# Three handovers in another order: one output-projection pass for two, a weight sum made one product earlier, and the retention's last two sweeps inside the norm's plan

## The chip, the cores and the metric

The kernel runs on one core of a Trainium2 chip. The metric is the device time of one execution in microseconds; the kernel before took 2762.98 us (median of three runs, 2762.88 to 2763.43).

## What is computed

A two-layer decoder trunk over 1024 positions of width 1024, in float32. Cut to what matters here:

```python
# layer 0: dilated attention beside a gated short convolution
x = x + concat([attention, conv_mixer], -1) @ even_w_out
x = x + ffn(rms_norm(x, ffn_norm[0]), 0)
# layer 1: retention with an output gate
x = x + (silu(xn @ wg) * group_norm(retention(q, k, v))) @ ret_wo
x = x + ffn(rms_norm(x, ffn_norm[1]), 1)

def ffn(xn, l):                       # D_FF = 2816
    u = causal_dwconv(xn @ w_up[l], conv_w[l])      # width 3
    g, val = split(u, 2, axis=-1)
    return (silu(g) * val) @ w_down[l]
```

So the products that the change touches are the output projection of layer 0, FFN 0's and 1's first block and down product, and the retention's output projection.

## The kernel before

**Numbers.** Every matmul operand is two float32r parts, high and low. `split` (L107) makes them: ScalarE (ACT) casts the high part (L109), and GpSimd (POOL) or VectorE (DVE) subtracts it for the low part (L110). `hilo` puts both parts in a buffer "hl" (7 of them) or in one that is passed in. `PASSES` (L47) lists the three matmuls that one product of parts takes. The residual x stays in SBUF as `xb`, eight row tiles of 128 positions.

**The output projections.** `sweep` (L296) goes over row tiles and the two halves of 512 columns: per pair of parts of the contraction three matmuls (L303) into one of four PSUM banks "o", then one addition of the bank to `xb` on DVE (L308). It yields after every row tile, so two additions. `project` (L568) is a sweep over the mixer's parts `mix[j]`; parts (1,3) and (5,7) ran earlier, beside the attention. `wo_sweep` (L1082) is one for a head of the retention; g is the half of the head's value dimension.

**The norms.** `Norming.play` walks a plan, a string of steps. "q2" makes the sums of squares of row-tile pair 2 (ACT L163, then the reciprocal root on POOL, L152 and L153); "r2" makes its normed rows in tiles "u" (DVE L172, two pieces of 512 per row tile, four per pair); "t2" turns them with PE (L179, sixteen transposes into four banks "b"); "c2" combines them into seven operand tiles `xc` (`combine`, L184: one ACT copy, L196 to L201 and three L110 on DVE, four L110 on POOL). "a", "A" and "b", "B" are the halves of a "q" and an "r". "s", "d" and "h" advance something else: "s" a sweep by two row tiles, "d" a sweep or the down product by so many steps, "h" the first FFN block by so many of its products. `PLAN` stands in front of FFN 0, `PLAN_DOWN` at the end of FFN 0's down product, `PLAN_LATE` in front of FFN 1.

**The FFN.** A block is `strassen` (L206): seven products (L220) over seven `xc` operands instead of eight; the first block runs in two halves of 256 columns so that it can start while later pairs are still being normed. The convolution (L892) of the first block follows it. The down product is `down_steps` (L719): five groups of 11 steps (products 1 and 2, 5 and 6, 3 and 7, 4, and the second half of 4), each step loading weight rows into "raw" buffers (5), making sums on DVE (L758), splitting, and multiplying (L826); a group ends with additions to `xb` (L834). The loop loads 4 steps ahead and makes operands 2 ahead.

**What sets the order.** The Python order of these calls gives each instruction its place, and a list scheduler puts the instructions on each engine's queue, which runs in that order. Buffers of one tag are reused when free, and a later user waits. DMA loads go out on SyncE (SP), stores on ACT's queue.

**The retention.** `last_block` (L1098) is the last projection block, with the first unit's loads, rotations (L979) and transposes between its products. Scores are L1012, masked with the tile "tri" on DVE (L1017). `gated` (L1068) turns a unit's output, multiplies it by the gate and splits it for `wo_sweep`.

## Time and profile before

| | us |
|---|---|
| profiled execution, device time | 2762.86 |
| its span, first to last instruction | 2761.1 |
| PE busy | 2675.4 |
| DVE busy | 1953.2 |
| ACT busy | 1191.6 |
| POOL busy | 754.2 |
| mean granted TensorE clock | 0.988 |

Between the profiled execution's time and its span lie 1.8 us. How to read what follows: a row of the timeline gives the start and length in us of a run of instructions of one kind, the engine, the source line, the operation, output and inputs by tile name, how many, and in brackets how long the engine had idled before it and what ended that idle time. A row of the windows gives, for a stretch of the span, the busy time of each engine with its number of instructions, the clock that TensorE was granted (1.00 is full), and the DMA engines' busy share. PE stands for TensorE's matmuls and PEld for its weight loads.

### The profile page before, as it was taken

To read this page: it belongs to the slowest core of one execution; us is meant where nothing else is said; L and a number is where in the kernel's file an instruction comes from. 1 tells how busy PE (TensorE), PEld (TensorE's weight loads), DVE (VectorE), ACT (ScalarE), POOL (GpSimd) and SP (SyncE) were. 2 spreads that over 40 slices of the span, in tenths; PEclk is the share of its full clock that TensorE was granted. 3 is DMA by queue.
4 is the path that set the end of the run, shared out by engine and by line. 5 is a ranking of instruction groups with operands and counts; after the bars stand their busy time and mean duration, and the time that the engine had idled before them with its cause. 6 is when DMAs were issued, how large, how long until landed. Compare 5 with 4: busy or idle time off the path is not lost.

```text
span 2761.1 us, 33920 instructions
## 1 busy us (share of the span) xinstructions
PE 2675.4 (97%) x12249; PEld 2151.1 (78%) x12249; DVE 1953.2 (71%) x2930; ACT 1191.6 (43%) x2030; POOL 754.2 (27%) x619
## 2 busy tenths in 40 slices
PE   8999999889999999989999999999998999999999
PEld 6877777678888877867888887788877888887887
DVE  4247676788787888785444435888778878787886
ACT  4344453355454444363333333333325545444444
POOL 6721113342222200033212122555555222221000
PEclk9999999999999999999999999999999999999999
DMA  5310002022222264433333335544321222224636
GB/s 170 102 47 28 24 31 80 27 78 76 86 75 87 74 244 160 138 118 117 103 111 103 111 104 175 167 158 137 100 77 50 78 86 75 87 74 168 210 122 212
DMA packets 250268, 294.73 MB, mean 107 GB/s; under 512 B 14288, under 2 KB 169076, under 8 KB 250100
## 3 DMA queue, kind: packets, MB, share of 16 engines
q1 hardware_dynamic: 233676, 238.55, 27.5%
q10 hardware_dynamic: 16424, 54.01, 5.1%
q8 instruction: 96, 1.57, 0.2%
q14 instruction: 72, 0.59, 0.1%
HBM read 234.31 MB, written 58.20 MB: 106 GB/s over the span
## 4 chain that ended last, share of the span: by engine, by line
PE 75%; DVE 12%; POOL 5%; issue 3%; DMA 3%; ACT 2%; SPq 0%; DVEq 0%; POOLq 0%; ACTq 0%
PE o L220 23%; PE b L220 22%; PE o L826 7%; PE b L826 6%; PE u L433 4%; PE n L382 2%; PE u L382 2%; PE o L303 2%; POOL hl L110 2%; DVE xb L308 2%; PE pv L503 1%; PE u L303 1%; PE s L472 1%; PE pt L515 1%; DVE u L172 1%
## 5 line engine op out<-in xcount | busy, mean ns | idle before, releaser
L110 POOL TENSOR_TENSOR hl<-raw,hl 128x512 fp32r<-128x512 f32 x347 | 499.3, 1448 | 1316.7 <-ACT hl L109 1293.4
L220 PE MATMUL b<-xc,hl 128*128 128x512 f32 (+1 forms) x2988 | 684.1, 388 | 1.4 <-POOL xc L110 0.9
L220 PE MATMUL o<-xc,hl 128*128 128x512 f32 (+1 forms) x2904 | 672.8, 391 | 10.3 <-ACT u L275 3.0
L220 PEld LDWEIGHTS b<-xc,hl 128*128 128x128 f32 x2988 | 548.5, 188 | 130.2 <-POOL xc L110 1.2
L220 PEld LDWEIGHTS o<-xc,hl 128*128 128x128 f32 x2904 | 537.9, 191 | 136.9 <-ACT u L275 3.6
L110 DVE TENSOR_TENSOR hl<-s,hl 128x512 fp32r<-128x512 f32 x325 | 225.1, 696 | 359.1 <-ACT hl L109 359.1
L109 ACT CAST hl<-raw 128x512 fp32r<-128x512 f32 (+1 forms) x424 | 257.9, 612 | 428.7 <-PE o L303 79.5
L892 DVE SCALAR_TENSOR_TENSOR u<-u,cc,u 128x1022 f32<-128x1022 f32 (+1 forms) x176 | 303.2, 1744 | 1.1
L109 ACT CAST hl<-s 128x512 fp32r<-128x512 f32 x325 | 199.7, 619 | 154.4 <-PE b L220 42.5
L433 PE MATMUL u<-xT,hl 128*128 128x512 f32 x576 | 172.8, 416 | 0.0
L308 DVE TENSOR_TENSOR xb<-xb,o 128x512 f32<-128x512 f32 x176 | 114.9, 678 | 21.9 <-PE o L303 21.6
L433 PEld LDWEIGHTS u<-xT,hl 128*128 128x128 f32 x576 | 99.4, 192 | 23.8 <-issue 9.5
L890 ACT ACTIVATE u<-u,cc 128x1024 f32<-128x1024 f32 x88 | 101.1, 1151 | 38.5 <-DVE u L287 30.2
L826 PE MATMUL o<-hl,hl 128*128 128x512 f32 x444 | 110.7, 393 | 2.4 <-DVE hl L110 1.6
L303 PE MATMUL o<-hl,ya 128*128 128x512 f32 x384 | 97.8, 406 | 5.1 <-DVE xb L308 5.1
L826 PEld LDWEIGHTS o<-hl,hl 128*128 128x128 f32 x444 | 83.0, 188 | 23.0 <-DVE hl L110 3.4
L893 ACT ACTIVATE u<-u 128x1024 f32<-128x1024 f32 x44 | 46.7, 1062 | 110.3 <-DVE u L892 110.2
L303 PEld LDWEIGHTS o<-hl,ya 128*128 128x128 f32 x384 | 73.4, 194 | 22.2 <-DVE xb L308 5.4
L152 POOL TENSOR_SCALAR rr<-ss 128x1 f32<-128x1 f32 (+1 forms) x48 | 13.4, 279 | 269.5 <-ACT s L163 250.5
L303 PE MATMUL o<-hl,yb 128*128 128x512 f32 x336 | 81.2, 397 | 0.0
L826 PE MATMUL b<-hl,hl 128*128 128x512 f32 x312 | 76.5, 392 | 1.1 <-DVE xb L834 1.0
L110 POOL TENSOR_TENSOR xc<-u,xc 128x512 fp32r<-128x512 f32 x48 | 66.4, 1411 | 35.7 <-DVE u L199 19.8
(207 smaller groups left out, 4011.8 us busy)
## 6 DMA issues: line engine op xcount, KB each, us to landing
raw<-in_ffn_w_up SPq DMA_DIRECT2D x176, 256.0 KB, 3.1
raw<-in_ffn_w_down SPq DMA_DIRECT2D x176, 256.0 KB, 3.1
scr<-u ACTq DMA_DIRECT2D x48, 512.0 KB, 2.8
hs<-u ACTq DMA_DIRECT2D x44, 512.0 KB, 2.7
h<-hs SPq DMA_DIRECT2D x44, 512.0 KB, 5.9
raw<-in_even_w_in SPq DMA_DIRECT2D x73, 256.0 KB, 2.9
raw<-in_ret_wo SPq DMA_DIRECT2D x64, 256.0 KB, 3.0
xb<-in_x SPq DMA_DIRECT2D x16, 512.0 KB, 3.2
```

What stands on the lines that cost most here:

```text
L109: act.copy(hi, src)
L110: (eng or pool).tensor_tensor(lo, src, f(hi), ALU.subtract)
L172: dve.scalar_tensor_tensor(xn[:, cs], xt[:, cs], r, g[i], ALU.mult, ALU.mult)
L220: pe.matmul(u, hl[:, ws, k * P : (k + 1) * P], xc[b][:, xs, k, cols_], start=(first and k == 0 and i == 0), stop=(k == 3 and i == 2), skip ...
L303: pe.matmul(o, lhs[j](ls, t), ws[j][hf][:, w, :], start=(j == 0 and i == 0), stop=(j == n - 1 and i == 2),)
L308: dve.tensor_tensor(xs, xs, o, ALU.add)
L382: pe.matmul(banks[t], xT[:, xs, k, t0 : t0 + P], hl[:, ws, :], start=(k == 0 and i == 0), stop=(k == KT - 1 and i == 2),)
L433: pe.matmul(u, hl(ws, k), xT[:, xs, k, hf * 512 : (hf + 1) * 512], start=(k == 0 and i == 0), stop=(k == KT - 1 and i == 2),)
L826: pe.matmul(o, l[:, ls, c * P : (c + 1) * P], r[:, ws, :], start=(start and i == 0), stop=(stop and i == 2), skip_group_check=True,)
L890: act.mul(c, u, wcol(2, jj))
L892: dve.scalar_tensor_tensor(c[:, d:], u[:, :-d], wcol(2 - d, jj), c[:, d:], ALU.mult, ALU.add)
L893: act.activation(cs[0], cs[0], AF.Silu)
```

## The change

It has five parts.

1. The plan strings are written in another order.
2. Layer 0's output projection runs passes (0,2), then (4,6) inside `PLAN`; before, (0,2) and (4,) ran by themselves and (6,) inside `PLAN`. The part `mix[4]` now lives in two "u" tiles, and "u" has five buffers instead of four.
3. In the down product the sum t4 = b21 − t4, its weight load and its store move from the group of product 4 into that of products 3 and 7. Two steps of product 4 share one "hl" buffer for their quarter-width operands, their t4 splits use "hl" buffers only, and from the third group's end on operands are made three steps ahead.
4. The last unit's gated output goes into an "h" tile and two "u" tiles, and both of its sweeps run inside `PLAN_LATE`, advanced by "d"; before, the first of them ran ahead of the plan.
5. The tile "tri" comes from the norm's "g" buffers, which are free earlier than its old place.

```diff
...
-PLAN = "s0 q0 s1 q1 r0 t0 s2 q2 c0 r1 t1 s3 q3 c1 r2 t2 c2 r3 h4 t3 c3 h4"
-PLAN_LATE = "t0 c0 s2 q2 t1 s3 q3 c1 r2 t2 c2 r3 t3 h4 c3 h4"
+PLAN = "s0 q0 s1 q1 r0 t0 s2 q2 c0 r1 s3 q3 t1 c1 h1 r2 t2 h1 c2 r3 h1 t3 h1 c3 h4"
+PLAN_LATE = "d1 t0 d1 c0 r1 d1 t1 d1 c1 d2 q2 h1 r2 d1 t2 d1 q3 h1 c2 r3 h1 t3 h1 c3 h4"
...
-    for js in ((0, 2), (4,)):
-        run(project(js, ORDER, o_bank))
+    run(project((0, 2), ORDER, o_bank))
...
-    nrm.play(PLAN, xc, project((6,), ORDER, o_bank), head[0])
+    nrm.play(PLAN, xc, project((4, 6), ORDER, o_bank), head[0])
...
-            return rhs(1, 1, k), rhs(0, 1, k)
...
+            return rhs(1, 1, k), rhs(0, 1, k), rhs(1, 0, k)
...
+            p7 = both(s3), both(t3)
             t4 = left[k][:, :HALF]
             add(t4, b21, t4, ALU.subtract)
-            p4 = quarter(right[k][:, HALF : HALF + 256]), both(t4)
             act.dma_start(out=ts[k], in_=t4)
-            return [p4]
+            return [p3, p7]
...
+            if k % 2 == 0:
+                pair.append(wp.tile([P, 2, 512], "hl", HL, F32R))
+            hl = pair[-1][:, :, k % 2 * 256 : k % 2 * 256 + 256]
...
+            while made_to[0] < min(n + AHEAD + (n >= 3 * KH), len(steps) - 1):
...
+        if last:
+            t = h_tile()
+            yT = [t[:, :, i * HALF : (i + 1) * HALF] for i in range(2)]
+            yT += [u_tile().bitcast(F32R).rearrange("p (s t) -> p s t", s=2) for _ in range(2)]
...
-        unit0["tri"] = rt[0].tile([P, HALF], "tri")
+        unit0["tri"] = wk.tile([P, HALF], "g", 2)
...
-            nrm.play("q0 r0 q1 r1")
+            nrm.play("q0 r0 q1")
...
-    run(wo_sweep(half, h, yT, 0, ORDER[4:]))
...
-    nrm.play(PLAN_LATE, xc, wo_sweep(half, h, yT, 1, ORDER[4:]), head[0])
+    nrm.play(PLAN_LATE, xc, chain(*[wo_sweep(half, h, yT, g, ORDER[4:]) for g in range(2)]), head[0])
```

What this does to the queues shows at three places. The first is DVE's queue in front of FFN 0 in the kernel before, from the seventh addition of pass (6,): `o` are banks of the projection, `u` normed rows, `rr` reciprocal roots, `b` banks of transposes.

```order
684 L308 TENSOR_TENSOR xb_71<-xb_71,o_4975 128x512
685 L308 TENSOR_TENSOR xb_71<-xb_71,o_4980 128x512
686 L172 SCALAR_TENSOR_TENSOR u_4997<-xb_71,rr_4956,g_4919 128x512
687 L172 SCALAR_TENSOR_TENSOR u_4997<-xb_71,rr_4956,g_4920 128x512
688 L172 SCALAR_TENSOR_TENSOR u_5000<-xb_71,rr_4962,g_4919 128x512
689 L172 SCALAR_TENSOR_TENSOR u_5000<-xb_71,rr_4962,g_4920 128x512
690 L308 TENSOR_TENSOR xb_71<-xb_71,o_5023 128x512
691 L308 TENSOR_TENSOR xb_71<-xb_71,o_5028 128x512
692 L308 TENSOR_TENSOR xb_71<-xb_71,o_5033 128x512
693 L308 TENSOR_TENSOR xb_71<-xb_71,o_5038 128x512
694 L196 TENSOR_TENSOR u_5055<-u_5056,b_5003 128x512
695 L198 TENSOR_TENSOR u_5056<-b_5018,u_5056 128x512
```

In the changed kernel the same queue at the same point of the norm, with the banks of pass (4,6):

```order
665 L308 TENSOR_TENSOR xb_71<-xb_71,o_4870 128x512
666 L172 SCALAR_TENSOR_TENSOR u_4942<-xb_71,rr_4889,g_4830 128x512
667 L308 TENSOR_TENSOR xb_71<-xb_71,o_4878 128x512
668 L172 SCALAR_TENSOR_TENSOR u_4942<-xb_71,rr_4889,g_4831 128x512
669 L308 TENSOR_TENSOR xb_71<-xb_71,o_4898 128x512
670 L172 SCALAR_TENSOR_TENSOR u_4945<-xb_71,rr_4895,g_4830 128x512
671 L308 TENSOR_TENSOR xb_71<-xb_71,o_4906 128x512
672 L172 SCALAR_TENSOR_TENSOR u_4945<-xb_71,rr_4895,g_4831 128x512
673 L308 TENSOR_TENSOR xb_71<-xb_71,o_4914 128x512
674 L308 TENSOR_TENSOR xb_71<-xb_71,o_4922 128x512
675 L196 TENSOR_TENSOR u_5012<-u_5013,b_4948 128x512
676 L198 TENSOR_TENSOR u_5013<-b_4963,u_5013 128x512
```

The normed rows of pair 0 stood together between additions of pass (6,); now they alternate with the additions of the merged pass, and combining tile 0 (L196 is its first step on DVE) comes after eight additions of the last pass instead of twelve.

The second place is PE's queue near the end of FFN 0's down product, before: the second tile's transposes among the steps of product 4 (the bank `o` and the operand buffers name the step).

```order
1715 L826 MATMUL o_8521<-hl_10421,hl_10418 128x512 x3
1716 L826 MATMUL o_8522<-hl_10421,hl_10418 128x512 x3
1717 L826 MATMUL o_8521<-u_10437,u_10434 128x512 x3
1718 L826 MATMUL o_8522<-u_10437,u_10434 128x512 x3
1719 L826 MATMUL o_8521<-hl_10494,hl_10491 128x512
1720 L826 MATMUL o_8522<-hl_10494,hl_10491 128x512
1721 L826 MATMUL o_8521<-hl_10494,hl_10491 128x512 x2
1722 L826 MATMUL o_8522<-hl_10494,hl_10491 128x512 x2
1723 L179 MATMUL b_10535<-ident_67,u_10349 128x128 x4
1724 L179 MATMUL b_10540<-ident_67,u_10367 128x128 x4
1725 L179 MATMUL b_10545<-ident_67,u_10349 128x128 x4
1726 L179 MATMUL b_10550<-ident_67,u_10367 128x128 x4
```

And in the changed kernel:

```order
1723 L833 MATMUL o_8490<-hl_10409,hl_10406 128x512 x3
1724 L833 MATMUL o_8491<-hl_10409,hl_10406 128x512 x3
1725 L833 MATMUL o_8490<-hl_10445,hl_10406 128x512
1726 L833 MATMUL o_8491<-hl_10445,hl_10406 128x512
1727 L179 MATMUL b_10501<-ident_67,u_10333 128x128 x4
1728 L179 MATMUL b_10506<-ident_67,u_10336 128x128 x4
1729 L179 MATMUL b_10511<-ident_67,u_10333 128x128 x4
1730 L179 MATMUL b_10516<-ident_67,u_10336 128x128 x4
1731 L833 MATMUL o_8490<-hl_10445,hl_10406 128x512 x2
1732 L833 MATMUL o_8491<-hl_10445,hl_10406 128x512 x2
```

The operands now come from "hl" buffers alone, one of them (`hl_10406`) serving two steps. Behind these transposes 34 matmuls of the down product remain, where 30 remained before.

The third place is DVE's queue in front of FFN 1, before: the eight pieces of normed rows of pairs 0 and 1 between the additions of two sweeps.

```order
2192 L308 TENSOR_TENSOR xb_71<-xb_71,o_17313 128x512
2193 L172 SCALAR_TENSOR_TENSOR u_17340<-xb_71,rr_17334,g_17321 128x512
2194 L172 SCALAR_TENSOR_TENSOR u_17340<-xb_71,rr_17334,g_17322 128x512
2195 L172 SCALAR_TENSOR_TENSOR u_17355<-xb_71,rr_17346,g_17321 128x512
2196 L172 SCALAR_TENSOR_TENSOR u_17355<-xb_71,rr_17346,g_17322 128x512
2197 L172 SCALAR_TENSOR_TENSOR u_17358<-xb_71,rr_17352,g_17321 128x512
2198 L172 SCALAR_TENSOR_TENSOR u_17358<-xb_71,rr_17352,g_17322 128x512
2199 L308 TENSOR_TENSOR xb_71<-xb_71,o_17381 128x512
2200 L308 TENSOR_TENSOR xb_71<-xb_71,o_17389 128x512
```

And in the changed kernel:

```order
2175 L308 TENSOR_TENSOR xb_71<-xb_71,o_17273 128x512
2176 L172 SCALAR_TENSOR_TENSOR u_17297<-xb_71,rr_17288,g_17282 128x512
2177 L172 SCALAR_TENSOR_TENSOR u_17300<-xb_71,rr_17294,g_17281 128x512
2178 L172 SCALAR_TENSOR_TENSOR u_17300<-xb_71,rr_17294,g_17282 128x512
2179 L308 TENSOR_TENSOR xb_71<-xb_71,o_17388 128x512
2180 L308 TENSOR_TENSOR xb_71<-xb_71,o_17396 128x512
2181 L196 TENSOR_TENSOR u_17440<-u_17441,b_17404 128x512
2182 L198 TENSOR_TENSOR u_17441<-b_17419,u_17441 128x512
2183 L199 TENSOR_TENSOR u_17440<-b_17419,u_17440 128x512
```

Four pieces instead of eight stand ahead of the first additions of the last unit's sweeps (`o_17388` is the first of them, as `o_17381` was), and combining tile 0 begins behind two of their additions instead of eight.

More of the change, by code (lines that the diff above doesn't have):

```diff
@@ L561, in gather @@
         for j in js:
-            hl = into.tile([P, 2, T], "h" if j == 6 else f"ab{j}", dt=F32R)
-            split(hl[:, 0, :], hl[:, 1, :], xb[:, j, :] if src is None else src, dve if j in (1, 5, 0, 6) else None)
+            if j == 4:
+                hl = [mix["mp"].tile([P, T], "u", 5, F32R) for _ in range(2)]
+            else:
+                t = into.tile([P, 2, T], "h" if j == 6 else f"ab{j}", dt=F32R)
+                hl = [t[:, s, :] for s in range(2)]
+            split(*hl, xb[:, j, :] if src is None else src, dve if j in (1, 5, 0, 6) else None)
             mix[j] = hl
@@ L569, in project @@
         return sweep(
-            [lambda s, t, h=mix[j]: h[:, s, t * P : (t + 1) * P] for j in js],
+            [lambda s, t, h=mix[j]: h[s][:, t * P : (t + 1) * P] for j in js],
             [w_rows(w_out, (j // 2) + (4 if j % 2 else 0)) for j in js], tiles, bank, after,
@@ L657, in u_tile @@
     def u_tile():
-        return mp.tile([P, T], "u", 4)
+        return mp.tile([P, T], "u", 5)
     def h_tile():
@@ L706, in tile @@
         def tile(shape, tag, bufs):
-            return (mp if tag == "u" else wk).tile(shape, tag, bufs)
+            return u_tile() if tag == "u" else wk.tile(shape, tag, bufs)
     xc = xc_tiles()
@@ L748, in hl_tile @@
                 return wp.tile([P, 2, 512], "hl", HL, F32R)
-            return mp.tile([P, 2, 512], "u", 4, F32R)
+            return mp.tile([P, 2, 512], "u", 5, F32R)
         def both(src, eng=dve):
@@ L793, in make_37, with quarter, make_4 @@
             t3 = add(s_tile(), b22, b12, ALU.subtract)
-            return [p3, (both(s3), both(t3))]
-        def quarter(src):
-            hl = hl_tile()
-            split(hl[:, 0, :256], hl[:, 1, :256], src, dve)
+            p7 = both(s3), both(t3)
+            t4 = left[k][:, :HALF]
+            add(t4, b21, t4, ALU.subtract)
+            act.dma_start(out=ts[k], in_=t4)
+            return [p3, p7]
+        pair = []
+        def quarter(src, k):
+            if k % 2 == 0:
+                pair.append(wp.tile([P, 2, 512], "hl", HL, F32R))
+            hl = pair[-1][:, :, k % 2 * 256 : k % 2 * 256 + 256]
+            split(hl[:, 0, :], hl[:, 1, :], src, dve)
             return hl
         def load_4(k):
-            return (rhs(1, 0, k),)
-        def make_4(k, b21):
-            t4 = left[k][:, :HALF]
-            add(t4, b21, t4, ALU.subtract)
-            p4 = quarter(right[k][:, HALF : HALF + 256]), both(t4)
-            act.dma_start(out=ts[k], in_=t4)
-            return [p4]
+            return ()
+        def make_4(k):
+            return [(quarter(right[k][:, HALF : HALF + 256], k), hilo(left[k][:, :HALF], None, dve))]
         def load_4b(k):
@@ L818, in make_4b @@
         def make_4b(k, t4, a22):
-            return [(quarter(a22[:, :256]), both(t4))]
+            return [(quarter(a22[:, :256], k), hilo(t4, None, dve))]
         x, y = [o_bank() for _ in range(4)], [b_bank() for _ in range(4)]
@@ L1068, in gated @@
     def gated(h, y, gt, last):
-        yT = [yp.tile([P, 2, 2, HALF], "ya", dt=F32R)]
-        yT.append(
-            h_tile().rearrange("p s (c t) -> p s c t", c=2) if last else yp.tile([P, 2, 2, HALF], "yb", dt=F32R)
-        )
+        if last:
+            t = h_tile()
+            yT = [t[:, :, i * HALF : (i + 1) * HALF] for i in range(2)]
+            yT += [u_tile().bitcast(F32R).rearrange("p (s t) -> p s t", s=2) for _ in range(2)]
+        else:
+            t = [yp.tile([P, 2, 2, HALF], f"y{i}", dt=F32R) for i in range(2)]
+            yT = [t[c // 2][:, :, c % 2] for c in range(4)]
         for c in range(4):
@@ L1083, in lhs @@
         def lhs(j):
-            return lambda s, t: yT[g][:, s, j, (t - 4 * half) * P : (t - 4 * half + 1) * P]
+            return lambda s, t: yT[2 * g + j][:, s, (t - 4 * half) * P : (t - 4 * half + 1) * P]
         return sweep(
```

15 lines of the change are left out of this document (7 added, 8 removed).

## The prediction

> **What bounds the kernel now.** I read the page first, then busy time by window, the waits of TensorE (PE), and the timelines of PE and VectorE (DVE) in the stages that wait.
>
> ```profile
> span 2761.1 us, 33920 instructions
> ...
> PE 2675.4 (97%) x12249; PEld 2151.1 (78%) x12249; DVE 1953.2 (71%) x2930; ACT 1191.6 (43%) x2030; POOL 754.2 (27%) x619
> ...
> L308 DVE TENSOR_TENSOR xb<-xb,o 128x512 f32<-128x512 f32 x176 | 114.9, 678 | 21.9 <-PE o L303 21.6
> ```
>
> PE is busy for 2675.4 of 2761.1 us. The change keeps all of its matmuls, so nothing can be won where PE never pauses. The rows below give, for each stretch: PE, PE load, DVE, ACT and POOL busy time, then the granted TensorE clock, the DMA share and GB/s.
>
> ```profile
> 510.00:590.00 80.00, 62.80 (x347) 54.76 (x346) 75.87 (x108) 37.20 (x70) 35.09 (x36) 0.85 0.15 44
> 540.00:560.00 20.00, 13.50 (x64) 12.04 (x64) 17.80 (x24) 8.58 (x17) 9.12 (x10) 0.58 0.05 14
> 640.00:680.00 40.00, 40.00 (x172) 32.18 (x171) 32.13 (x35) 19.08 (x28) 9.71 (x6) 1.00 0.26 83
> 1080.00:1120.00 40.00, 40.00 (x176) 32.63 (x175) 37.58 (x63) 17.57 (x30) 0.00 (x0) 1.00 0.46 147
> 1120.00:1160.00 40.00, 40.00 (x175) 32.65 (x174) 28.32 (x46) 16.38 (x29) 0.00 (x0) 1.00 0.30 99
> 1196.00:1269.00 73.00, 58.35 (x330) 47.46 (x329) 64.15 (x96) 41.37 (x84) 33.27 (x27) 0.93 0.33 98
> 1220.00:1240.00 20.00, 16.56 (x76) 12.55 (x77) 19.18 (x29) 12.18 (x25) 8.48 (x6) 0.85 0.48 142
> 1700.00:1760.00 60.00, 52.20 (x248) 41.83 (x247) 47.86 (x69) 26.86 (x43) 31.30 (x26) 0.94 0.64 224
> 2055.00:2128.00 73.00, 59.84 (x343) 52.55 (x343) 64.72 (x93) 37.68 (x72) 40.05 (x38) 0.88 0.17 48
> ```
>
> The steady FFN stretch (640 to 680) is plain PE work: 172 matmuls in 40.00 us, 0.2325 us each. Four stretches are not: the norm in front of FFN0 (510 to 590, PE idle 17.2 us), the handover from FFN0's down product to the retention projections (1196 to 1269, 14.7 us), the entry to the retention (1700 to 1760, 7.8 us) and the norm in front of FFN1 (2055 to 2128, 13.2 us). Together they hold 52.8 of PE's 85.7 idle us. In the first, DVE is busy for 75.87 of 80 us: DVE's list sets that stage's length.
>
> **The change, part by part.** *Norm in front of FFN0.* Passes (4,) and (6,) of the output projection become one pass (4,6). Each pass adds 16 tiles into xb on DVE (L308); 48 additions become 32, and the matmuls stay. These are DVE's and PE's rows there:
>
> ```profile
> 511.72 16.42 DVE L308 TENSOR_TENSOR xb<-xb,o 128x512 f32<-128x512 f32 x25
> 528.05 2.73 DVE L172 SCALAR_TENSOR_TENSOR u<-xb,rr,g 128x512 f32<-128x512 f32 x4
> 530.70 2.47 DVE L308 TENSOR_TENSOR xb<-xb,o 128x512 f32<-128x512 f32 x4
> 533.09 0.68 DVE L196 TENSOR_TENSOR u<-u,b 128x512 f32<-128x512 f32 x1
> ...
> 536.75 1.80 DVE L172 SCALAR_TENSOR_TENSOR u<-xb,rr,g 128x512 f32<-128x512 f32 x1
> ...
> 544.88 0.68 DVE L196 TENSOR_TENSOR u<-u,b 128x512 f32<-128x512 f32 x1
> ...
> 557.69 0.69 DVE L196 TENSOR_TENSOR u<-u,b 128x512 f32<-128x512 f32 x1 [2.20 <-ACT u L195]
> ...
> 569.60 0.68 DVE L196 TENSOR_TENSOR u<-u,b 128x512 f32<-128x512 f32 x1
> ...
> 590.20 2.48 DVE L892 SCALAR_TENSOR_TENSOR u<-u,cc,u 128x1023 f32<-128x1023 f32 x2
> ```
>
> ```profile
> 521.66 7.60 PE L303 MATMUL o<-hl,h 128*128 128x512 f32 x32
> ...
> 530.47 1.47 PE L179 MATMUL b<-ident,u 128*128 128x128 f32 x12
> ...
> 538.70 0.63 PE L179 MATMUL b<-ident,u 128*128 128x128 f32 x4 [3.95 <-DVE u L172]
> 541.96 2.82 PE L179 MATMUL b<-ident,u 128*128 128x128 f32 x12 [2.63 <-DVE u L172]
> 546.66 0.58 PE L220 MATMUL o<-xc,hl 128*128 128x256 f32 x1 [1.88 <-ACT xc L109]
> ```
>
> Four additions from 530.70 end where L196 starts at 533.09: 2.39 us, 0.60 each when DVE is not held. The 25 at 511.72 begin with the last addition of pass (0,2), which both orders have, so this is a common anchor. Combining tile 1 starts at 544.88, 33.16 us behind it, with 33 additions, 8 pieces of normed rows and 7 pieces of combining tile 0 between. In the changed order the same span holds 17 additions, the same 15 other pieces and two more pieces of weight work: 16 × 0.60 less, 2 × 0.60 more, so −8.4 us. Two things must not hold DVE back. PE: pass (6,) starts at 521.66 and pass (4,) is 48 matmuls, so pass (0,2) ended near 521.66 − 48 × 0.2325 = 510.5; 96 matmuls from there end at 532.8, before the 536.5 that DVE's sum gives. And the pieces that stand behind one another: with six matmuls per addition (1.40 us against 0.60) DVE has 0.8 us free per tile beside the pass, into which the rows and the first combine fall. Further on, the 2.20 us in which DVE waited for ACT ahead of combining tile 2 should be filled, since rows, sums and splits of FFN weights have moved ahead: −2.2. Sum −10.6. Nothing gained (0 of the 2.2, a further 2 us held by the split that gives back the u buffers) is −6; all 4.1 us of DVE's idle gone and the additions at 0.68 (16 × 0.68 + 4.1) is −15. The fifth u buffer is there because mix[4] occupies two of them to the end of the pass; if r1's second row must wait for the POOL split of tile 0, that is inside the −6.
>
> *FFN0's down product.* The sum t4 = b21 − t4 moves from the fourth product to the third, with its load on SP and its store on ACT. DVE then does seven pieces per step there instead of six, at about 0.6 us in a step of 24 × 0.2325 = 5.58 us. The window at 1080 has three loads per step and DVE at 37.58 of 40 us with PE at 40.00; the one at 1120 has two and 28.32. So room exists: cost 0, up to +2. In the fourth product one DVE piece per step goes, but two steps share a buffer.
>
> The handover after it has a shorter way to tile 0 (transposes one step earlier) and rows spread between down steps:
>
> ```profile
> 1215.35 0.66 PE L179 MATMUL b<-ident,u 128*128 128x128 f32 x4 [1.19 <-DVE xc L110]
> 1216.95 0.63 PE L179 MATMUL b<-ident,u 128*128 128x128 f32 x4 [0.94 <-DVE xc L110]
> 1218.60 0.76 PE L179 MATMUL b<-ident,u 128*128 128x128 f32 x4 [1.03 <-DVE xc L110]
> ...
> 1228.01 1.19 PE L826 MATMUL o<-hl,hl 128*128 128x512 f32 x4 [1.55 <-DVE hl L110]
> ...
> 1252.23 1.98 PE L179 MATMUL b<-ident,u 128*128 128x128 f32 x12 [2.28 <-DVE u L172]
> ```
>
> DVE's list is nearly the same length; it is idle for 73 − 64.15 = 8.9 us of this stretch. The three waits of tile 1 come to 3.2 us; the new order puts less between tile 0's rows and its combine, but more after. I take −2, with −5 (all 3.2 and most of the 2.28) and +2 (shared buffers hold a split) as ends.
>
> *Entry to the retention.* The triangle's load comes earlier, and three score matmuls now stand among the last projection block's matmuls.
>
> ```profile
> 1720.50 2.32 DVE L110 TENSOR_TENSOR qk<-kf,qk 128x1024 fp32r<-128x1024 f32 x1
> ...
> 1725.63 3.92 PE L1012 MATMUL b<-qk,qk 128*128 128x512 f32 x24
> ```
>
> They need what DVE finishes at 1722.8; with 24 matmuls (5.6 us) behind them they would be reached near 1720, so PE may stop for 2.8 us, or win it back as the scores end sooner. I take 0, ends −2 and +3.
>
> *Norm in front of FFN1.* One of the last two passes of the retention's output projection ran before the norm, with eight pieces of normed rows ahead of its additions on DVE. Both passes now run inside the plan.
>
> ```profile
> 2060.25 1.41 DVE L172 SCALAR_TENSOR_TENSOR u<-xb,rr,g 128x512 f32<-128x512 f32 x2 [0.44 <-POOL rr L153]
> 2062.11 3.41 DVE L172 SCALAR_TENSOR_TENSOR u<-xb,rr,g 128x512 f32<-128x512 f32 x2 [0.44 <-POOL rr L153]
> 2065.44 2.47 DVE L308 TENSOR_TENSOR xb<-xb,o 128x512 f32<-128x512 f32 x4
> ```
>
> ```profile
> 2066.17 8.66 PE L303 MATMUL o<-hl,ya 128*128 128x512 f32 x24 [5.13 <-DVE xb L308]
> ...
> 2076.11 5.83 PE L303 MATMUL o<-hl,h 128*128 128x512 f32 x24
> ...
> 2101.18 1.09 PE L179 MATMUL b<-ident,u 128*128 128x128 f32 x4 [4.16 <-DVE u L172]
> 2104.44 2.82 PE L179 MATMUL b<-ident,u 128*128 128x128 f32 x12 [2.17 <-DVE u L172]
> ```
>
> PE stopped for 5.13 us because no bank was free, and the 24 matmuls behind it took 8.66 instead of 5.83 us: 8.0 us. Here no DVE work goes; DVE's idle time, 73 − 64.72 = 8.3 us, is all that can be won without shortening its list. I take −7, ends −4 (the later sum of squares of pair 3 leaves a wait near tile 3) and −11 (the halved clock behind 4.16 goes too).
>
> Other edits (POOL's orders, the tag names, the earlier buffers) lie beside PE at 40.00 in its windows: 0. Sum: −10.6 − 2 + 0 − 7 ± 0 = −19.6, about −20 us. The profiled run took 2762.86 us, 0.12 under the median of 2762.98; the forecast is 2743. The best ends give −15 − 5 − 2 − 11 = −33, the worst −6 + 2 + 2 + 3 − 4 = −3.
>
> The clock deserves a look: 540 to 560 ran at 0.58, behind stalls of 3.95 and 2.63 us. The Trainium skill, TensorE: Matmul & The Clock Gate, section "What's actually happening", says that PE's clock halves after about 3.4 us of idleness in a free-running window and comes back after about as long of busy work. The trace agrees only in part: at 1220 to 1240 the clock fell to 0.85 where the longest stall is the 1.55 us at 1228.01. By the rule, shortening these stalls below its window would keep the full clock; that is a rival.
>
> **The rivals.** *(a) DVE takes it back.* The stage in front of FFN0 stays DVE's, and a reordered list idles elsewhere (r1 behind the POOL split; 536.75 shows a piece at 1.80 us instead of 0.68 beside POOL). Then only the low ends come: −6 − 0 − 4 = −10, 2753. For: the long stalls in front of both FFNs name L172, not a bank.
>
> *(b) The clock stays up.* In 510 to 590 the clock is 0.85 and in 2055 to 2128 it is 0.88; at half speed that is 2 × 0.15 × 80 = 24 and 2 × 0.12 × 73 = 17.5 us, on work worth half as much at full clock. Most of it lies behind DVE's list. Twelve transposes took 1.47 us at 530.47 and 2.82 at 541.96. The loss is at most half of 41.5, 20.8; as DVE's list covers part of it, I count half, −10 more: 2733. By the rule of the Trainium skill above the result would be this one. Against: the clock also fell among short stalls at 1220.
>
> *(c) Slower: the third load starves the third product.* A step needs three of the shared raw buffers. If each of 22 steps (both layers) waited for a transfer by 2 us, that is +44, less the 20: 2787. It decides once a step waits for over 0.9 us. Against: the second product has three loads per step and PE 40.00.
>
> *(d) Nothing moves.* Gains at the handovers return at the next stage, which is bound otherwise (DMA 0.64 at the retention entry): 2763 ± 5. Against: behind the first norm PE is at 40.00 in 40 us, so an earlier start there is an earlier end.
>
> **How the numbers follow.** Forecast 0.66; (a) 0.14; (b) 0.09; (c) 0.05; (d) 0.06. Differences under 0.2% (5.5 us) cannot be told from none. Faster: 0.66 + 0.14 + 0.09 less what of (a) falls short, 0.02, gives 0.87; same 0.08; slower 0.05. The range of 8 in 10 leaves out (c), (d) and the outermost of (b) and of (a): 2731 to 2757.
>
> **What would show it.** Right: L308 with 160 additions instead of 176; combining of tiles 1, 2 and 3 earlier by 8 to 11 us against the anchor; 5.13 gone near 2066; each later stage shifted by the running sum, −11, −13, −13, −20. Wrong: PE below 40.00 in the third down product, L179 stalls as long as before, a new wait for the score matmuls of over 3 us, or the shift behind one handover lost in the next.

## The result and the profile after

The changed kernel took 2748.12 us (median of four runs, 2746.10 to 2749.78) against 2762.93 for the kernel before: a ratio of 0.9947, 95% interval 0.9932 to 0.9963. That is 14.8 us faster; 20 were forecast, and the time lies inside the range. The sum came out near its forecast by luck in part: two of its terms were wrong by about 5 us each, in opposite directions, and a third by 3. Most of what follows is about those. One of the 11 executions of the kernel with the fifth u buffer took 5130.37 us, and no ratio below counts it.

The page of the changed kernel has PE's matmuls unchanged in number, and 160 additions on L308 for 176:

```profile
span 2744.3 us, 33784 instructions
...
PE 2669.2 (97%) x12249; PEld 2147.1 (78%) x12249; DVE 1894.3 (69%) x2914; ACT 1185.8 (43%) x2030; POOL 829.9 (30%) x619
...
L308 DVE TENSOR_TENSOR xb<-xb,o 128x512 f32<-128x512 f32 x160 | 104.5, 678 | 19.1 <-PE o L303 19.1
```

The windows of the same stages, moved to where they now lie (the norm in front of FFN 0, the steady stretch, the second and the third group of the down product, the entry to the retention, the norm in front of FFN 1), with the same columns as before. The third group starts 12 us earlier here, so the last row is the kernel before at the place that 1120 to 1160 has in the changed one:

```profile
508.40:588.40 80.00, 68.33 (x378) 59.20 (x378) 70.99 (x96) 39.62 (x75) 39.88 (x38) 0.89 0.15 44
640.00:680.00 40.00, 40.00 (x172) 32.19 (x171) 30.21 (x36) 19.50 (x29) 13.84 (x6) 1.00 0.25 79
1080.00:1120.00 40.00, 40.00 (x175) 32.40 (x174) 34.92 (x58) 16.48 (x29) 0.00 (x0) 1.00 0.52 163
1120.00:1160.00 40.00, 40.00 (x176) 32.63 (x175) 29.17 (x48) 16.12 (x29) 0.00 (x0) 1.00 0.60 186
1690.00:1750.00 60.00, 50.11 (x231) 39.26 (x230) 43.43 (x68) 24.69 (x42) 30.26 (x25) 0.94 0.64 228
2045.00:2118.00 73.00, 64.41 (x373) 54.32 (x373) 67.27 (x97) 41.29 (x77) 45.00 (x40) 0.98 0.17 48
```

```profile
1132.00:1172.00 40.00, 40.00 (x175) 32.66 (x174) 25.00 (x40) 15.73 (x28) 0.00 (x0) 1.00 0.49 158
```

The reader is to see three things. In front of FFN 0 DVE is busy for 70.99 of 80 us where it was 75.87: the list became shorter, but DVE idles 9.0 us where it idled 4.1. The third down group (1120) carries more transfers, 186 GB/s for 158, and more work on DVE, 29.17 us for 25.00, and PE still stands at 40.00. In front of FFN 1 the clock went from 0.88 to 0.98.

Stages are compared by the start of the same matmul in two traces (the n-th of a source line; 12249 are recorded in each). In the table each column is the time from one such matmul to another, in us. *Norm 0* runs from the 291st of the sweeps to the 501st of the FFN and projection blocks; *down a* is the first group of FFN 0's down product and *down A* that of FFN 1 (264 matmuls each); *handover* runs from the 791st down matmul to the 2101st block matmul; *entry* from the 3501st block matmul to the 421st sweep matmul; *norm 1* from the 1041st sweep matmul to the 4501st block matmul; *tail* from the 1715th down matmul to the end. All other stretches agree within 0.5 us in every kernel, except the start (507 to 511, nothing there was changed) and the second down group, which came out at 62 instead of 60.7 in two profiles (the fifth u buffer with the down part, and the changed kernel's second).

| kernel | norm 0 | down a | handover | entry | norm 1 | down A | tail | span |
|---|---|---|---|---|---|---|---|---|
| before | 154.1 | 64.6 | 82.2 | 180.7 | 144.6 | 64.0 | 36.9 | 2761.1 |
| before, again | 153.5 | 64.5 | 84.0 | 182.2 | 143.8 | 64.4 | 37.2 | 2760.4 |
| triangle moved | 153.2 | 64.8 | 84.1 | 183.9 | 144.5 | 63.8 | 37.0 | 2761.9 |
| late sweeps in the plan | 153.2 | 65.1 | 86.7 | 180.8 | 137.8 | 63.4 | 37.2 | 2756.1 |
| fifth u buffer | 153.3 | 61.7 | 83.4 | 183.5 | 142.3 | 61.7 | 36.6 | 2752.3 |
| fifth u buffer, down part | 154.6 | 61.3 | 79.6 | 185.8 | 143.5 | 62.2 | 39.7 | 2759.8 |
| merged pass, new plan | 148.0 | 62.2 | 83.8 | 185.8 | 143.5 | 62.4 | 37.6 | 2755.6 |
| merged pass, old plan | 146.7 | 61.6 | 83.1 | 183.6 | 142.8 | 61.6 | 37.1 | 2747.5 |
| changed | 147.7 | 61.1 | 82.2 | 183.3 | 137.4 | 62.3 | 37.8 | 2744.3 |
| changed, again | 148.0 | 62.2 | 79.7 | 185.5 | 137.5 | 61.2 | 39.2 | 2746.3 |
| changed, additions back | 155.7 | 61.7 | 81.5 | 183.4 | 137.5 | 61.5 | 38.3 | 2751.1 |
| changed, scores behind | 147.7 | 61.9 | 81.6 | 179.7 | 137.5 | 60.9 | 39.1 | 2741.5 |
| the same, old plan | 146.7 | 62.2 | 82.7 | 179.8 | 137.5 | 61.6 | 38.9 | 2740.4 |
| the same, old sums too | 146.2 | 61.1 | 84.3 | 181.1 | 137.5 | 61.7 | 35.6 | 2740.5 |

Norm 0, down a, norm 1 and down A repeat within 1 or 2 us among kernels that are alike there; the handover scatters by up to 4.5, entry and tail by about 2, so that for these means over several rows are the better evidence. Each row is one execution, and its span need not be the kernel's median: the rows "fifth u buffer, down part", "merged pass, new plan" and "the same, old plan" show the longest of the executions timed, 3.5, 4.3 and 2.9 us over their medians.

### The profile page after: what moved, and what is told of

Read it like the earlier page. It is cut to its first block, busy times and chain, and to the rows that moved or that the text cites. A ratio compares the mean times of both kernels' runs of the same rounds, so it can differ in the third digit from the quotient of the medians.

```text
span 2744.3 us, 33784 instructions
## 1 busy us (share of the span) xinstructions
PE 2669.2 (97%) x12249; PEld 2147.1 (78%) x12249; DVE 1894.3 (69%) x2914; ACT 1185.8 (43%) x2030; POOL 829.9 (30%) x619
## 5 line engine op out<-in xcount | busy, mean ns | idle before, releaser
L110 POOL TENSOR_TENSOR hl<-raw,hl 128x512 fp32r<-128x512 f32 x347 | 574.5, 1669 | 1223.2 <-ACT hl L109 1213.3
L220 PE MATMUL o<-xc,hl 128*128 128x512 f32 (+1 forms) x2904 | 672.3, 391 | 14.8 <-ACT u L275 5.0
L110 DVE TENSOR_TENSOR hl<-s,hl 128x512 fp32r<-128x512 f32 x325 | 226.7, 701 | 390.1 <-ACT hl L109 389.8
L109 ACT CAST hl<-raw 128x512 fp32r<-128x512 f32 (+1 forms) x440 | 265.3, 609 | 424.8 <-issue 105.1
L900 DVE SCALAR_TENSOR_TENSOR u<-u,cc,u 128x1022 f32<-128x1022 f32 (+1 forms) x176 | 264.5, 1527 | 0.9
L303 PE MATMUL o<-hl,y 128*128 128x512 f32 x672 | 164.5, 397 | 0.0
L833 PE MATMUL o<-hl,hl 128*128 128x512 f32 x600 | 146.3, 394 | 4.9 <-DVE hl L110 3.5
L303 PEld LDWEIGHTS o<-hl,y 128*128 128x128 f32 x672 | 125.0, 188 | 29.0 <-DVE xb L308 0.5
L833 PEld LDWEIGHTS o<-hl,hl 128*128 128x128 f32 x600 | 111.1, 188 | 34.7 <-DVE hl L110 7.3
L308 DVE TENSOR_TENSOR xb<-xb,o 128x512 f32<-128x512 f32 x160 | 104.5, 678 | 19.1 <-PE o L303 19.1
L109 ACT CAST hl<-h 128x512 fp32r<-128x512 f32 (+1 forms) x108 | 60.1, 575 | 78.0 <-PE o L833 24.4
L110 POOL TENSOR_TENSOR xc<-u,xc 128x512 fp32r<-128x512 f32 x48 | 68.2, 1452 | 45.9 <-DVE u L199 32.8
L110 DVE TENSOR_TENSOR hl<-h,hl 128x512 fp32r<-128x512 f32 (+1 forms) x108 | 66.4, 632 | 18.8 <-ACT hl L109 18.5
```

The source lines that it names most:

```text
L109: act.copy(hi, src)
L110: (eng or pool).tensor_tensor(lo, src, f(hi), ALU.subtract)
L220: pe.matmul(u, hl[:, ws, k * P : (k + 1) * P], xc[b][:, xs, k, cols_], start=(first and k == 0 and i == 0), stop=(k == 3 and i == 2), skip ...
L303: pe.matmul(o, lhs[j](ls, t), ws[j][hf][:, w, :], start=(j == 0 and i == 0), stop=(j == n - 1 and i == 2),)
L308: dve.tensor_tensor(xs, xs, o, ALU.add)
L833: pe.matmul(o, l[:, ls, c * P : (c + 1) * P], r[:, ws, :], start=(start and i == 0), stop=(stop and i == 2), skip_group_check=True,)
```

## The experiments

The change comes apart into pieces, but some of its parts lean on each other in SBUF, the memory that holds the tiles. The pool "ab" of the kernel before holds seven parts of the mixer at 8 KB per partition each, and the triangle takes 2 KB of the retention's first pool. Parts 2 and 5 move `mix[4]` and the triangle to make room for the fifth u buffer, so the three are tried together; no run shows how much room it needs.

**The fifth u buffer alone** (with `mix[4]` in u tiles and the triangle moved; passes, plans and sums as before):

```diff
-            hl = into.tile([P, 2, T], "h" if j == 6 else f"ab{j}", dt=F32R)
+            if j == 4:
+                hl = [mix["mp"].tile([P, T], "u", 5, F32R) for _ in range(2)]
...
-        return mp.tile([P, T], "u", 4)
+        return mp.tile([P, T], "u", 5)
...
-        unit0["tri"] = rt[0].tile([P, HALF], "tri")
+        unit0["tri"] = wk.tile([P, HALF], "g", 2)
```

> The kernel before with the room part alone: the part mix[4] in two u tiles, five u buffers instead of four, and the triangle tile in the norm's g buffers; all passes, plans and sums as before. Theory A (the fifth u buffer serves the down products, whose splits wait for a free u tile): FFN 0's first two groups of the down product gain about 3.4 us and FFN 1's about 1.6, so about 2758, with nothing gained in front of FFN 0. Rival (those gains come from the t4 sum or the plans): 2763, no shift between the first down step and the third group. The entry to the retention, with the triangle moved, costs 2 to 3 us by both, so 2760 or 2765.

Measured: 2755.43 us, ratio 0.9977 (0.9968 to 0.9986). Norm 0 is unchanged (153.3); the first down group is 61.7 for 64.6, that of FFN 1 61.7 for 64.0. PE's waits in the first group point to the cause. This is the kernel before, around that group; three of the four rows, 1.7 us, are waits for splits into u tiles:

```profile
PE b L826 <- DVE xb L834: 1.0, 1, 1.0
PE o L826 <- ACT u L109: 0.9, 1, 0.9
PE b L826 <- ACT u L109: 0.5, 1, 0.5
PE b L826 <- DVE u L110: 0.3, 1, 0.3
```

And with the fifth buffer (L830 is the same matmul), the one wait that is left:

```profile
PE o L830 <- ACT u L109: 0.8, 1, 0.8
```

And ACT's own waits there, first before, then with the fifth buffer: the columns are total, times and longest in us. Before, casts into a u tile stood for 18.0 us in all behind matmuls that had still to read the tile, 5.6 at the longest; afterwards for 12.6, and 2.5 at the longest. ACT as a whole doesn't wait less: its casts into "hl" buffers stood behind PE for 6.4 us before (3.2 and 3.2) and for 14.6 afterwards. What became shorter is the longest wait for a single tile.

```profile
ACT u L109 <- PE o L826: 11.5, 4, 5.6
ACT u L109 <- PE b L826: 6.5, 5, 1.7
```

```profile
ACT hl L109 <- PE o L830: 9.0, 6, 2.2
ACT u L109 <- PE b L830: 7.1, 4, 2.5
...
ACT hl L109 <- PE b L830: 5.6, 4, 1.7
ACT u L109 <- PE o L830: 5.5, 4, 1.6
```

Theory A holds in place and, for the down groups, roughly in size; the time is lower than the 2760 that it came to with the triangle's cost. With the next experiment, in which the triangle alone leaves the down groups at 64.8 and 63.8, the gain there is the buffer's. The buffer has a side effect that costs PE nothing: the 347 weight splits on POOL (L110, hl<-raw) took 1.43 to 1.45 us on the mean in the four kernels with four u buffers and 1.66 to 1.67 in all with five, while the stretch from norm 0 to the first down step, FFN 0's other blocks, is 335.5 us in every one.

**The triangle alone** (one line, four u buffers):

```diff
-        unit0["tri"] = rt[0].tile([P, HALF], "tri")
+        unit0["tri"] = wk.tile([P, HALF], "g", 2)
```

> The kernel before with the triangle tile alone moved to the norm's g buffers, four u buffers. Theory A (the early score matmuls stop PE at the entry to the retention): a wait of 1.0 us or more for the low part of qk and 2 to 3 us later behind the entry, 2765. Rival (what the entry lost comes from something else that stands there, such as the loads or the clock): within 0.5 us, 2763.

Measured: 2765.10 us, ratio 1.0014 (1.0005 to 1.0023): slower by a little. The entry takes 183.9, against 180.7, 182.2 and 180.8 in the three kernels with the triangle in its old place. PE's timeline of this kernel at the entry:

```profile
1720.31 0.49 PE L1012 MATMUL b<-qk,qk 128*128 128x512 f32 x1 [1.01 <-DVE qk L110]
...
1735.00 6.66 PE L1038 MATMUL o<-v,ky 128*128 128x512 f32 x21 [2.38 <-DVE ky L1029]
1752.43 2.31 PE L998 MATMUL b<-ident,vt 128*128 128x128 f32 x8 [2.74 <-DVE ky L1064]
```

The first score matmuls stop PE for 1.01 us, and the waits behind are 2.38 and 2.74 where they were 2.10 and three short ones of 2.8 in all. Theory A holds: in none of the rows does the masking wait for the triangle's load, and yet moving it costs some 3 us, since PE's queue comes out in another order, with score matmuls among the block's.

**The merged pass with the new plan** (on top of the fifth u buffer):

```diff
-    for js in ((0, 2), (4,)):
-        run(project(js, ORDER, o_bank))
+    run(project((0, 2), ORDER, o_bank))
...
-    nrm.play(PLAN, xc, project((6,), ORDER, o_bank), head[0])
+    nrm.play(PLAN, xc, project((4, 6), ORDER, o_bank), head[0])
```

> The kernel of the fifth u buffer plus the merged pass (4,6) and the new plan in front of FFN 0, all else as before. Theory A (16 additions leave DVE's list, but the chain of rows, transposes and combining gives part of it back): the convolution of the first block 7 us earlier, 5 to 7 us left at the 40th us of FFN 0. Rival (the additions are worth their whole time, and the profiled run only fell short by chance): 10 us or more. Against the kernel before 2752 by the first, 2748 by the second.

Measured: 2753.16 us, ratio 0.9965 (0.9952 to 0.9979). Norm 0 falls from 153.3 to 148.0, by 5.3 us: theory A, in the stage and in the time.

**The merged pass with the old plan** (the same with the plan string of before):

> The merged pass with the old plan in front of FFN 0 (the fifth u buffer as before it). Theory A (the 16 additions that leave DVE are worth most, the order of the plan little): 4 to 5 of the 5.4 us that the merged pass with its new plan gained. Rival (the new order of the plan is what pays, since it fills DVE beside the pass): 2 us or less, 2755.

Measured: 2749.26 us, ratio 0.9951 (0.9939 to 0.9964). Norm 0 is 146.7, 6.6 us less than with separate passes. The merging pays all of the gain, more than theory A gave it; the new order of the plan takes 1.3 back. Norm 0 repeats this: 147.7 to 148.0 in four kernels with the new plan, 146.2 to 146.7 in three with the old one.

**The late sweeps alone** (parts 4 and `PLAN_LATE` on the kernel before, four u buffers):

```diff
-            nrm.play("q0 r0 q1 r1")
+            nrm.play("q0 r0 q1")
...
-    run(wo_sweep(half, h, yT, 0, ORDER[4:]))
...
-    nrm.play(PLAN_LATE, xc, wo_sweep(half, h, yT, 1, ORDER[4:]), head[0])
+    nrm.play(PLAN_LATE, xc, chain(*[wo_sweep(half, h, yT, g, ORDER[4:]) for g in range(2)]), head[0])
```

> The kernel before with the last unit's gated output in h and u tiles and both of its sweeps inside the plan in front of FFN 1, all else as before (four u buffers). Theory A (the 5.1 us stop for a bank and the half clock behind it are what the stage loses): 7 us, 2756. Rival (it needs the fifth u buffer, since two u tiles hold the output to the end of the sweeps): 2 us or less, 2761 or more, with long waits of the row pieces on u tiles.

Measured: 2755.34 us, ratio 0.9979 (0.9970 to 0.9987). Norm 1 takes 137.8 us for 144.6 and 143.8. The stop of 5.13 us is gone; the window from 2045 to 2125 has the clock at 1.00:

```profile
2045.00:2125.00 80.00, 70.20 (x409) 58.55 (x408) 73.65 (x110) 44.39 (x82) 45.88 (x45) 1.00 0.17 50
```

Theory A holds; the fifth u buffer isn't needed for this part.

**The additions put back as other work.** The changed kernel with one more DVE piece behind each addition of the merged pass:

```diff
                 dve.tensor_tensor(xs, xs, o, ALU.add)
+                if again:
+                    dve.tensor_tensor(xs, xs, xs, ALU.max)
```

> The changed kernel with 16 more pieces on DVE in the merged pass, each the larger of xb and itself (it changes nothing in the result), so that DVE's list is as long as in the kernel before. Theory A (DVE's list is only part of the stage's length now; DVE idles 9 of 80 us there while it waits for banks, reciprocal roots and PE's transposes): the stage in front of FFN 0 loses 2 to 5 us of the 16 × 0.6 = 9.6, about 2752. Rival (DVE's list sets the length as before): 8 us or more, 2757.

Measured: 2753.36 us, ratio to the kernel before 0.9967 (0.9956 to 0.9979). Norm 0 takes 155.7 for 147.7 and 148.0: 7.9 us of the 9.6 come back, 0.49 us a piece. By the stage, the rival's 8 us are met within 0.1 and my theory A fell: DVE's list does set its length for the most part, idle time in the changed kernel or not. The time alone does not say so: by the ratios the whole kernel lost some 4 to 6 us, and 2753.36 lies nearer to theory A's 2752 than to 2757. Also, each added piece writes `xb` between the addition and what reads it, so it delays the rows behind it as well as filling DVE. This is the group of the added pieces (L310) in that kernel between 505 and 560, count, busy time and mean in ns:

```profile
L310 DVE TENSOR_TENSOR xb<-xb 128x512 f32<-128x512 f32 x16 | 11.2, 728 | 0.1
```

**The down part** (on top of the fifth u buffer: the t4 sum in the third product, shared quarter buffers, operands three steps ahead, and the new `PLAN_DOWN`; its lines are those of the change):

> The kernel of the fifth u buffer plus the down product's part: the t4 sum in the third product, shared quarter buffers, operands three steps ahead from there, and the new plan at the handover to the retention. Theory A (the third product has room, the handover gains little): against the kernel of the fifth u buffer 0 in the third product, −1 to −3 at the handover, the same again at the end of FFN 1, so 2753. Rival (three loads per step starve the third product): PE below 40.00 of 40 us there and 5 us or more lost, 2760.

Measured: 2758.04 us, ratio 0.9987 (0.9978 to 0.9996). The handover falls from 83.4 to 79.6, and the tail of FFN 1 grows from 36.6 to 39.7. The third group's own stretch takes 60.6 us for 60.3, so it isn't starved. In front of it PE stops once, for DVE's additions and not for a load, and in the tail it waits for casts into "hl" buffers; these are PE's waits in the two places, and what those casts wait for themselves:

```profile
PE b L834 <- DVE xb L842: 1.3, 1, 1.3
```

```profile
PE o L834 <- ACT hl L109: 2.0, 5, 0.9
```

```profile
ACT hl L109 <- DMA raw<-hs: 9.1, 5, 3.2
ACT hl L109 <- PE o L834: 5.7, 5, 2.1
```

Theory A was right on the third product, and on the handover as far as one row shows it. It was wrong on the end of FFN 1, where it expected the gain of the handover again: there the part loses. And it was wrong on the time: 2758.04 lies 5 us over its 2753 and 2 under the rival's 2760, though the rival's starved product isn't there. Beside the fifth buffer alone (0.9977, 0.9968 to 0.9986) the part gains nothing that the times show.

**The scores behind the block.** The changed kernel with the first unit's scores in the banks that the block uses:

```diff
-    def scores(q, k):
+    def scores(q, k, bank=b_bank):
...
-            b = b_bank()
+            b = bank()
...
-        sT = scores(q, k)
+        sT = scores(q, k, b_bank if n else o_bank)
```

> The changed kernel with the first unit's scores in the o banks instead of the b banks, which puts most of the score matmuls behind the last projection block's and the key rows' transposes ahead of its end. Theory A (the entry to the retention loses its time because the first score matmuls stop PE for qk and everything behind follows): 2 to 4 us earlier behind the entry than the changed kernel, 2745. Rival (the entry waits for the key rows and the loads whatever the order of PE): within 1 us, 2748.

Measured: 2743.14 us, ratio 0.9932 (0.9919 to 0.9944). The entry takes 179.7 for 183.3 and 185.5. PE's timeline of this kernel:

```profile
1704.53 0.66 PE L1035 MATMUL b<-ident,kf 128*128 128x128 f32 x4 [0.48 <-POOL kf L996]
...
1711.59 3.07 PE L220 MATMUL o<-xc,hl 128*128 128x512 f32 x12 [1.63 <-DVE v L1008]
...
1718.25 3.02 PE L1020 MATMUL o<-qk,qk 128*128 128x512 f32 x20
1721.10 5.66 PE L1046 MATMUL o<-v,ky 128*128 128x512 f32 x24
```

The stop for qk and the one of 2.38 us for the key rows are gone: the transposes of the key rows (L1035) now run at 1704 and 1709, inside the block, so that the state's matmuls (L1046) follow the scores at once. Theory A's 2 to 4 us came as 3.6 and 5.8 beside the two profiles of the changed kernel, and the time as 2743 for 2745. But the edit did two things: it moved the scores back and the key rows forward. Which share each has, no run tells.

**Second profiles of both kernels.**

> The changed kernel again, for a second profile of each stage and a time on the same chip as the two kernels below. If the stage ledger of the first profile holds: 6 to 7 us at the norm in front of FFN 0, 3 in the first two down groups, 0 at the handover to the retention, a loss of 2 to 3 at its entry, 7 at the norm in front of FFN 1, 2748. Rival (the profiles of one kernel differ by several us per stage, so that the ledger is chance): shifts that differ by over 2 us in two or more stages.

> The kernel before again, for a second profile of each stage. If its first profile is typical, every stage's length agrees within 1 us, the handover to the retention apart, where unchanged kernels came out 1 to 4 us longer than in the first profile. Rival: the first profile was slow in front of FFN 0 by chance (the controls were 1 us shorter there), and the merged pass is worth less than the ledger says.

Measured: 2748.45 us, ratio 0.9951 (0.9937 to 0.9964), for the changed kernel; the columns of the table agree with the first profile within 1.1 us but for the handover (79.7 for 82.2), the entry (185.5 for 183.3) and the tail (39.2 for 37.8). The kernel before, in one execution, took 2762.17 us; it differs from its first profile by 1.8 us at the handover, 1.5 at the entry, and by 0.8 or less in the other columns. So those three columns carry chance of 2 us, as the rival feared, and a single difference there is a hint and no proof.

**Two versions put together.** Both have the scores behind the block, the merged pass and the old plan; the second also has the t4 sum back in the fourth product.

```diff
-PLAN = "s0 q0 s1 q1 r0 t0 s2 q2 c0 r1 s3 q3 t1 c1 h1 r2 t2 h1 c2 r3 h1 t3 h1 c3 h4"
+PLAN = "s0 q0 s1 q1 r0 t0 s2 q2 c0 r1 t1 s3 q3 c1 r2 t2 c2 r3 h4 t3 c3 h4"
```

> The changed kernel with the old plan in front of FFN 0 (with the merged pass) and the first unit's scores in the o banks. Theory A: 4 to 5 us under the changed kernel, 2744, and 1 us over the kernel with the old sums. Rival (the old plan's 1 us was chance): 3 us under it, 2745.

> The changed kernel with three things otherwise: the old plan in front of FFN 0 (with the merged pass), the first unit's scores in the o banks, and the t4 sum back in the fourth product with its own quarter buffers. Theory A (the old plan is worth 1 us there, the scores behind the block 3 to 4, the sums in their old place 1 us at the end): 5 us under the changed kernel, 2743. Rival (the moved sum frees DVE for the handover and pays there): 3 us under it or less, and behind the next kernel.

Measured: 2739.32 us, ratio 0.9920 (0.9907 to 0.9932), with the moved sum, and 2742.24, ratio 0.9926 (0.9914 to 0.9939), with the sums in their old place. The first is clear of the changed kernel on the same chip (0.9951, 0.9937 to 0.9964). For the second the intervals just touch, though none of its executions (2740.87 to 2743.07) reaches one of the changed kernel's (2745.53 to 2750.92). Between the two the intervals overlap as well; the medians favour the moved sum by 2.9 us, against theory A, but that is not shown. In the two profiles what the moved sum wins at the handover (82.7 for 84.3) it gives back in the tail (38.9 for 35.6). Their spans, 2740.4 and 2740.5, are no fair pair, though: the first is the longest of that kernel's five executions. Theory A on the old sums is not borne out. The second version also takes back the shared quarter buffers and the third step ahead, so it tries the three together.

## Why the prediction was right in the sum, point by point

By means over the rows that are alike: norm 0 fell from 153.7 (six kernels with separate passes) to 147.9 (four with the merged pass and the new plan), −5.8. The first down groups fell from 64.8 to 61.7 and from 63.9 to 61.7, −5.3 in all. The handover went from 83.9 to 81.2, −2.7; the entry from 181.2 to 184.4, +3.1; norm 1 from 143.6 to 137.5, −6.1; the tail from 37.1 to 38.8, +1.7. The sum is −15.1; the timed difference is −14.8. The sign that each later stage would be shifted by −11, −13, −13 and −20 did not come in these sizes: the running sum is −5.8 behind norm 0, −11.6 behind the handover, −8.5 behind the entry and −14.6 behind norm 1. What the handover won was lost at the entry, which the prediction had named as a sign of being wrong.

**In front of FFN 0: −10.6 forecast, −5.8 measured.** The count and the place were right: 16 additions left DVE, and DVE's list is what they left. The size was off. The step that failed is "Two things must not hold DVE back", and with it the 2.2 us that "should be filled": the two things were PE and the order of the pieces, and what held DVE were POOL and ACT. These are DVE's rows of the changed kernel; the anchor is the addition at 510.16:

```profile
510.16 0.67 DVE L308 TENSOR_TENSOR xb<-xb,o 128x512 f32<-128x512 f32 x1
...
514.76 0.75 DVE L172 SCALAR_TENSOR_TENSOR u<-xb,rr,g 128x512 f32<-128x512 f32 x1 [0.76 <-POOL rr L153]
...
518.25 0.75 DVE L172 SCALAR_TENSOR_TENSOR u<-xb,rr,g 128x512 f32<-128x512 f32 x1 [0.88 <-POOL rr L153]
...
523.35 0.69 DVE L196 TENSOR_TENSOR u<-u,b 128x512 f32<-128x512 f32 x1 [1.89 <-ACT u L195]
...
529.93 3.77 DVE L172 SCALAR_TENSOR_TENSOR u<-xb,rr,g 128x512 f32<-128x512 f32 x4
...
536.67 0.69 DVE L196 TENSOR_TENSOR u<-u,b 128x512 f32<-128x512 f32 x1
...
543.45 4.76 DVE L172 SCALAR_TENSOR_TENSOR u<-xb,rr,g 128x512 f32<-128x512 f32 x4
...
550.75 0.69 DVE L196 TENSOR_TENSOR u<-u,b 128x512 f32<-128x512 f32 x1 [0.79 <-ACT u L195]
...
561.47 0.67 DVE L196 TENSOR_TENSOR u<-u,b 128x512 f32<-128x512 f32 x1
...
578.17 0.69 DVE L249 TENSOR_TENSOR s<-raw,raw 128x512 f32<-128x512 f32 x1 [1.96 <-DMA raw<-in_ffn_w_up]
```

And these are rows of the kernel before: the rest of pair 1's normed rows, and two FFN sums that stood between tiles 2 and 3:

```profile
539.07 3.49 DVE L172 SCALAR_TENSOR_TENSOR u<-xb,rr,g 128x512 f32<-128x512 f32 x3
...
566.58 0.68 DVE L250 TENSOR_TENSOR s<-s,raw 128x512 f32<-128x512 f32 x1
567.18 0.68 DVE L251 TENSOR_TENSOR s<-raw,raw 128x512 f32<-128x512 f32 x1
```

Combining tile 1 starts 26.5 us behind the anchor (536.67 − 510.16), where it was 33.2 and 24.8 was forecast. On the way DVE now waits for reciprocal roots (0.76, 0.88) and for ACT's copy (1.89), waits that the longer list had covered, while the four row pieces of pair 1 took 3.77 us instead of 1.80 and 3.49. Tile 2 starts 14.1 us after tile 1 (12.8 before): the wait for ACT fell from 2.20 to 0.79 us, but the two FFN sums now stand here, beside POOL's splits, and took 1.50 and 1.17 us instead of 0.68 each, and DVE waits 0.73 us for a product of PE. Tile 3 then starts 10.7 us after tile 2 (11.9 before). Against the anchor the three tiles are 6.7, 5.4 and 6.6 us earlier, where 8 to 11 were named as the sign of being right. The wait at 578.17, for a weight load, is longer than the 1.05 us that stood there before. So the waits came back under other names; rival (a) described this stage. Of the shortfall 1.3 us is the new plan's: with the old string the merged pass won 7.1 (153.7 to the mean of 146.7, 146.7 and 146.2).

The additions are worth less than 0.60 us each: 7.9 us for sixteen when put back, 0.49 each.

**The down products: 0 forecast, −5.3 measured.** The step that failed is "Other edits (… the earlier buffers) lie beside PE at 40.00 in its windows: 0". The windows that it rested on began at 1080; the waits lie between 1000 and 1070, at the start of the product, where operands are made against the buffers that the first steps still hold. I costed the fifth buffer for the norm only and never looked at its other users. The forecast for the third product, 0 with +2 at worst, held (60.3 to 60.6 us in all kernels, and in two of the twelve down products with the moved sum a stop of 1.0 and 1.3 us in front of it, for DVE's additions), and rival (c) is out. The prediction's reading of the window 1120 to 1160 was 6 us early, since the third group starts at 1126: in the group itself DVE stood at 25.00 of 40 us, not 28.32, so there was more room than I took.

**The handover: −2 forecast, −2.7 measured; the reason is open.** I had put the gain to the new order, and the waits for combining that it counted did shrink: from 3.2 and 2.8 us in the two profiles of the kernel before to 1.5 and 1.6 in those of the changed one. But PE's waits for normed rows, 3.5 and 2.4 before, are 3.5 and 4.1, and with the new plan and the old sums the handover came out at 84.3, as long as before. So what pays there may be the t4 sum, taken off DVE, or the shared buffers or the operands made a step earlier, which that experiment took back with it. It is one experiment, in a column that scatters by several us: nothing is shown. What the part won came back in the tail (+1.7), which the prediction had at zero: there PE waits for casts into "hl" buffers, and whether it is the sharing or the loads that holds these, no run tells.

**The entry: 0 forecast, ends −2 and +3; +3.1 measured.** The mechanism was in the text, at its upper end: "PE may stop for 2.8 us". The stop itself was 1.00, and 2.73 stood behind it, in the changed kernel:

```profile
1710.24 0.50 PE L1020 MATMUL b<-qk,qk 128*128 128x512 f32 x1 [1.00 <-DVE qk L110]
...
1724.91 6.67 PE L1046 MATMUL o<-v,ky 128*128 128x512 f32 x21 [2.38 <-DVE ky L1037]
...
1742.34 0.66 PE L1006 MATMUL b<-ident,vt 128*128 128x128 f32 x4 [2.73 <-DVE ky L1072]
```

The triangle alone reproduces it, and a change of the banks takes it back: 179.7 and 179.8 us, for 181.2 with the triangle in its old place.

**In front of FFN 1: −7 forecast, −6.1 measured.** Here the reading was right in place, cause and size. The stop of 5.13 us is gone, and the sweep's 48 last matmuls run at full pace, 11.34 us, 0.236 each, where 24 had taken 8.66:

```profile
2061.05 1.09 PE L179 MATMUL b<-ident,u 128*128 128x128 f32 x8 [1.04 <-DVE u L172]
...
2063.92 11.34 PE L303 MATMUL o<-hl,u 128*128 128x512 f32 x48
```

**Rival (b), the clock,** came true at one of its two places. In front of FFN 1 the longest stall of PE is now 2.09 us and the clock 0.98 (1.00 with the late sweeps alone); in front of FFN 0 a stall of 3.27 us is left and the clock is 0.89. The rule of the Trainium skill (TensorE: Matmul & The Clock Gate, "What's actually happening"), a halved clock after some 3.4 us of idleness, agrees with the long stalls of the kernel before (3.95 us in front of FFN 0, 5.13 in front of FFN 1), and with the 3.27 us if "some" is taken widely. It does not account for the rest: in the changed kernel the clock stood at 0.50 from 2088 to 2091.4, where the longest stall is the 2.09 us, and in the kernel before at 0.51 from 1219 to 1226, behind waits of at most 1.19 us (the 1.55 us that the prediction named came after the fall). The gain of rival (b) did not come on top, though: the 2.8 us that the halved clock had cost behind 2066 were already in the −7.

The direction did not hang on the split: but for rival (c), which did not come, every mechanism I had for a loss was small. But the nearness of 2743 to 2748 is luck in good part: it owes much to −5.3 that I had not seen.

## What to carry to other kernels

When a change adds a buffer to make room for something, look up every user of that buffer's tag, and the waits at the start of each: here it was worth as much as the edit it was made for. Work taken off a saturated engine is worth less than its time where other waits lie just beneath, so cost the next wait on that engine's queue too, and test it by putting the time back as work that changes nothing. And a load that nothing waits for can still cost: here its new place came with another order on PE, so read the queues of every engine for rows that moved though no line of them was edited.
